# GpSimd makes the folded Fourier input of the second layer, and the first rotary product runs behind the next q's evictions

## The chip, the cores and the metric

The kernel runs on one core of a Trainium2 chip. Its engines are TensorE (PE, with weight loads listed apart as PEld), VectorE (DVE), ScalarE (ACT), GpSimd (POOL) and SyncE (SP, which here only issues DMAs). Each engine works through its own list of instructions in order; semaphores hold an instruction back until what it reads is there. The metric is the device time of one execution, in microseconds (us).

## The reference, cut to what matters

Two layers of an encoder over 272 tokens (16 learned meta tokens and 256 others) with 2048 channels, in float32. Of a layer, the change touches only the way into the projection `f` and into the queries:

```python
h = rmsnorm(x, norm_mix[i])
proj = h @ w_in[i]                      # columns q | k | v | f | ga | gf
q, k: per-head RMS norm over 128 channels, then 2-D rotary:
    concat([x1 * c - x2 * s, x1 * s + x2 * c])      # on each half of the head
f = proj[..., OFF_F:OFF_GA]             # 1024 columns, 8 groups of 128
fr = fft2(f, axes=(tokens, group channels), norm="ortho").real
x = x + (sigmoid(ga) * attn_branch + sigmoid(gf) * (fr @ w_four)) @ w_out
x = x + conv_ffn(rmsnorm(x))
```

The real part of a transform over the tokens needs only the even and the odd part of its input about the middle. So the second layer projects for `f` not `h` but its sums and differences `h[n] + h[T-n]` and `h[n] - h[T-n]`, up to 138 columns each: the *folded* input (`fw` is the weight prepared for it in memory).

## The kernel before, in words

**Products in three parts.** Every weight streams from memory in chunks of 512 KB, tile `raw` (128 x 1024 numbers, four blocks of 128 contraction rows by 256 columns, or in `f4` one contraction block by 1024 columns), issued by SP (L264) into five buffers. Of each chunk ACT makes a rounded copy `wh` (L303) and DVE the remainder `wl` (L306, which waits for that copy); each has four buffers and is made up to three chunks ahead. The activations are split the same way, into `xH` and `xL`. PE adds up `wh*xH`, `wh*xL` and `wl*xH`. Nearly everything else is done in the shadow of these products.

**The order of the work.** Side work is written as Python generators on a list. At each step of the product loops the code takes the next piece of them: `yield n` means "go on in n steps", and `until(hold, flag)` runs them until a flag is set. A scheduler then fixes the order of instructions on each engine from that program, except where a stretch is marked `manual_schedule`; there the order is the one written. DVE has such a stretch around the second q chunk and the folded projection of layer 2, and ACT around that q's evictions and the folded projection.

**The order in layer 2** is k, v, q0, q1, f4, q2, q3 and the gates. `f4` is the folded projection: 16 contraction blocks (k = 0 to 15, chunks 448 to 463 from a weight named `fw`), on each of which PE runs products of `wh` and `wl` with the folded input of that block (L845, L849). Chunk 447 is the last of q1.

**The folded input.** `rstdB` is the tokens' normalising factor, broadcast over partitions; it is ready shortly before layer 2's v. Unit b of eight covers contraction blocks 2b and 2b+1 and has four operations: `t1 = XT * rstdB` (L781, 128 x 544 numbers), the sum (L783, 128 x 274), the difference (L784, 128 x 276), and a copy of the two unpaired columns (L785, 128 x 4). Then, for each block, ACT makes the rounded, scaled part (L788) and DVE its remainder (L795), in one of eight slots, five of which lie in tile `hA` and three in `hB`. Units 0 to 3 are made ahead, in the steps of v and q0 (`fold_ahead`); units 4 to 7 within f4 into slots that are then free, one in three blocks. `t1`, `hf` and most other scratch tiles of this stage (`qp`, `qps`, `qs`, `kp`, `kps`, and later `cf` and `sg`, the constants of the Fourier transform over channels) share one tag of seven buffers.

**Around the change.** `head_evac` empties a q or k product from PSUM (L912 on ACT for the squares, L913 on DVE, into `qp`). `swap` moves halves of heads about by four DMAs into `qs`. `rope` is three DVE products (L930 to L932), an ACT cast (L933) and a DVE subtraction (L935). `kstats` makes the keys' norm: sums by DVE into `kss` (L921, L956, L957), POOL's power `rk` (L515), six scalings `dk` by DVE (L964), and on PE a product of `dk` with ones, `ps_kb` (L967), that stands in PE's list ahead of the last products of v. `pn` are the attention's probabilities, which POOL scales later (L1086).

The manual stretch reads:

```python
                if last and i == 1:
                    until(hold, "ahead")
                    with tc.manual_schedule(engines={mybir.EngineType.DVE}):
                        ps = group((l, "q", i), xr(lo), W)
                        with tc.manual_schedule(engines={mybir.EngineType.Activation}):
                            qq = head_evac(ps, prm[:, P_QN + l:P_QN + l + 1], "qp", lo)
                            qq += (swap(qq[0]),)
                            folded_f(slots, E)
```

Of the kernel before, what the change touches and what calls it, by code (L numbers as in the profile page):

```python
# [13 lines left out]
ALU = mybir.AluOpType  # L14
# [6 lines left out]
T = NM + SEQ  # L21
DEPTH = 2
KT = D // P
# [54 lines left out]
TH = T // 2 + 2  # L78
# [100 lines left out]
def encoder_kernel(ctx, tc, xT, params, consts, bmat, cfold, csign, w_fl, w_f64c, w_in, w_abr, w_four, w_f64, w_out, w_up, w_down, w_vn, w_dn, w_dt, out):  # L179
    nc = tc.nc  # L180
# [12 lines left out]
    for l in range(DEPTH):  # L193
# [42 lines left out]
    for key, chs in order:  # L236
        for j, ch in enumerate(chs):
            n = 0
# [58 lines left out]
    def split_w(i, a, b, parts="hl"):  # L297
        if i not in splits:
            splits[i] = split_tiles(i)
        h, lo = splits[i]  # L300
        r = raws[i]
        if "h" in parts:
            nc.scalar.copy(h[:, a:b], r[:, a:b])  # L303
        st["wl"] = lo
        if "l" in parts:
            nc.vector.tensor_tensor(lo[:, a:b], r[:, a:b], h[:, a:b].bitcast(F32), op=ALU.subtract)  # L306
            if b == CW:
                del raws[i]
# [25 lines left out]
    def until(hold, flag):  # L334
        while flag not in hold:
            step(True)
# [173 lines left out]
    def bc2(ap):  # L510
        return _rep(ap, 2)
# [99 lines left out]
    for l in range(DEPTH):  # L611
# [4 lines left out]
        hold = {}  # L616

        with tc.tile_pool(name=f"mix{l}", bufs=1) as mp:
# [159 lines left out]

            def fold_sum(b, slots):
                t1 = rt("t1")  # L780
                nc.vector.tensor_tensor(t1, XT[:, 2 * b:2 * b + 2, :], bc2(rstdB), op=ALU.mult)  # L781
                hf = rw("hf").rearrange("p k (e n) -> p k e n", e=2)
                nc.vector.tensor_tensor(hf[:, :, 0, 1:TH], t1[:, :, 1:TH], t1[:, :, T - 1:T - TH:-1], op=ALU.add)  # L783
                nc.vector.tensor_tensor(hf[:, :, 1, :], t1[:, :, 1:TH + 1], t1[:, :, T - 1:T - TH - 1:-1], op=ALU.subtract)  # L784
                nc.scalar.copy(hf[:, :, 0, 0:T // 2 + 1:T // 2], t1[:, :, 0:T // 2 + 1:T // 2])  # L785
                for q in range(2):
                    k = 2 * b + q
                    nc.scalar.activation(slots[k % NS][:, :, 0, :], hf[:, q], AF.Copy, scale=prm[:, P_NM + l * KT + k:P_NM + l * KT + k + 1])  # L788
                return hf

            def fold_low(b, slots, hf):
                for q in range(2):
                    k = 2 * b + q
                    sl = slots[k % NS]
                    nc.vector.scalar_tensor_tensor(sl[:, :, 1, :], hf[:, q], prm[:, P_NM + l * KT + k:P_NM + l * KT + k + 1],  # L795
                                                   sl[:, :, 0, :].bitcast(F32), op0=ALU.mult, op1=ALU.subtract)

            def fold_ahead(slots):
                yield 9
                for b in range(NS // 2):  # L800
                    hf = fold_sum(b, slots)
                    yield 2
                    fold_low(b, slots, hf)
                    yield 1
                hold["ahead"] = True

            def folded_f(slots, E):
                assert order[st["grp"]][0] == (l, "f4")
                st["grp"] += 1
                ps = {}  # L810
                for g in (0, 1, 2, 3):
                    ps[g] = [psum.tile([P, 512], F32, tag="aux" if g < 2 else "mm", name=f"ps_f{g}{e}") for e in range(2)]
                p64 = ps[0][0][:2 * NG, 2 * TH:3 * TH]
                hf = None
                wx = {}
                for k in range(KT):
                    i = st["next"]
                    advance(i + 1 + LOOK)
                    ahead = [j for j, _ in todo]
                    todo.clear()  # L820
                    if k < KT - 1:
                        for j in ahead:
                            split_w(j, 0, CW, "h")
                    if hf is not None:
                        fold_low(hf[0], slots, hf[1])
                        hf = None
# [12 lines left out]
                    for q, g in kg:  # L839
                        h, lo_, sl = wx[q]  # L840
                        for e in range(2):
                            w = slice(e * P, (e + 1) * P)
                            o2 = st2(ps[g][e][:, :2 * TH].rearrange("p (r n) -> p r n", r=2))
                            x = al(sl[:, e])
                            nc.tensor.matmul(o2, h[:, g, w], x, start=q == 0, stop=False)  # L845
                            if g == e == 0:
                                for r in range(2):
                                    nc.tensor.matmul(p64, w64s[:, q, :], sl[:, 0, r, :], start=False, stop=False)
                            nc.tensor.matmul(st2(ps[g][e][:, :TH]), lo_[:, g, w], x[:, 0], start=False, stop=q == KT - 1)  # L849
                        if k == KT - 1:  # L850
                            for e in range(2):
                                ev = hv(E[:, g, e, :])
                                nc.scalar.copy(ev, de(ps[g][e][:, TH:2 * TH]))
                                nc.vector.tensor_tensor(ev, de(ps[g][e][:, :TH]), ev, op=ALU.add)
                            if g == 3:
                                for j in ahead:
                                    split_w(j, 0, CW)
                            if g == 0:
                                nc.scalar.copy(e64, p64)
# [66 lines left out]
                    tc.keep_in_program_order(nc.sync.dma_start(qs[32 * b:32 * b + 32, :, :], hp[32 * (b ^ 1):32 * (b ^ 1) + 32, :, :]))  # L926
                return qs

            def rope(hp, qs, H, L):
                tc.keep_in_program_order(nc.vector.tensor_tensor(qs, qs, bc2(sin), op=ALU.mult))  # L930
                tc.keep_in_program_order(nc.vector.tensor_tensor(hp, hp, bc2(cos), op=ALU.mult))
                nc.vector.tensor_tensor(hp, hp, qs, op=ALU.add)  # L932
                nc.scalar.copy(H, hp)  # L933
                yield 1
                nc.vector.tensor_tensor(L, hp, H.bitcast(F32), op=ALU.subtract)  # L935
# [77 lines left out]
            def q_stage(i, qp, qsq, qs):  # L1013
                kv, j = i // 2, i % 2
                sl = slice(2 * j, 2 * j + 2)
                if j == 0:
                    qvs.append(small.tile([P, 9], F32, tag="qv", name="qv"))
                    qsms.append(small.tile([P, 2, 4, NM], F32, tag="sqm", name="sqm", bufs=2))
                qv, qsm = qvs[kv], qsms[kv]
                yield 5  # L1020
                nc.vector.tensor_copy(qsm[:, :, 2 * j:2 * j + 2, :], qsq[:, :, 0:NM].unsqueeze(1).to_broadcast([P, 2, 2, NM]))
                d4 = qv[:, 4 * j:4 * j + 4]
                sums_t(d4, [qsq[:, m, a:b] for m in range(MG) for a, b in BLK[1:]])
                d4 = d4.rearrange("p (m i) -> p m i", m=2)
# [9 lines left out]
                yield from rope(qp, qs, qH[kv][:, sl, :], qL[kv][:, sl, :])  # L1034
# [536 lines left out]
```

## Time and profile before

| | |
|---|---|
| time, median of 3 runs | 2376.45 us (2375.04 to 2378.63) |
| profiled execution | 2377.1 us, span 2375.2 us, granted TensorE clock 0.999 |
| PE busy | 2357.5 us, 99% of the span |
| DVE, ACT, POOL busy | 1802.9, 1313.3, 191.5 us (76%, 55%, 8%) |
| memory traffic | 660.70 MB, mean 278 GB/s |

The profile is of one execution. The page gives the busy time of each engine; the lists of waits say how long an engine stood idle before an instruction and which engine's work ended that; timelines give start and duration of single instructions. A busy figure for PE says only that an instruction was running: at half the granted clock it is as busy and takes longer, so the tables by windows (sum of the window, then busy us and instruction count of PE, PEld, DVE, ACT and POOL, then the granted clock as a share of full speed, the busy share of the DMA engines, and GB/s) have to be read beside it.

### The profile page before, as it was taken

The page shows a single profiled execution, that of the slowest core. Times are in us where ns is not written, and L with a number is a line of the kernel's source. Part 1 is how long each engine was busy: PE and PEld are TensorE (multiplying, and loading weights), DVE is VectorE, ACT ScalarE, POOL GpSimd, SP SyncE. Part 2 cuts the span into 40 slices and gives each one's busy share as a digit, 9 for nine tenths or more (in the row PEclk, how much of TensorE's full clock was granted, in tenths as well). Part 3 has the DMA queues.
Part 4 walks back from the last instruction along what each step waited for, and adds up shares of the span by engine and source line. Part 5 has one row for each costly group of instructions (what it writes and reads, how often), then busy time and mean ns, then how long its engine had stood idle before and what let it go on. Part 6 is the DMA issues. An engine that isn't in the chain of part 4 may idle for free. (4 is left out here: it accounts for less than half of the span.)

```text
span 2375.2 us, 47690 instructions
## 1 busy us (share of the span) xinstructions
PE 2357.5 (99%) x18992; PEld 2305.7 (97%) x18992; DVE 1802.9 (76%) x2813; ACT 1313.3 (55%) x1929; POOL 191.5 (8%) x303
## 2 busy tenths in 40 slices
PE   9999999999999999999999999999999999999999
PEld 9999999999999999999999999999999999999998
DVE  7787867877777556767568877676888889888798
ACT  6565544554444334444455665445676666666575
POOL 0022110000000000000000131000010000000000
PEclk9999999999999999999999999999999999999999
DMA  7557999989999999999886546888889989988887
GB/s 268 178 165 229 305 297 318 294 285 337 319 316 309 320 325 328 309 322 310 263 261 202 182 151 217 263 287 256 285 303 307 323 291 307 306 305 282 258 283 264
DMA packets 171217, 660.70 MB, mean 278 GB/s; under 512 B 19425, under 2 KB 24673, under 8 KB 170097
## 3 DMA queue, kind: packets, MB, share of 16 engines
q1 hardware_dynamic: 152528, 538.07, 64.5%
q0 software_dynamic: 17024, 117.45, 19.7%
q8 instruction: 149, 2.44, 0.4%
q10 hardware_dynamic: 1440, 2.13, 0.3%
q14 instruction: 76, 0.61, 0.1%
HBM read 635.91 MB, written 136.31 MB: 325 GB/s over the span
## 5 line engine op out<-in xcount | busy, mean ns | idle before, releaser
L306 DVE TENSOR_TENSOR wl<-raw,wh 128x1024 fp32r<-128x1024 f32 (+1 forms) x937 | 1129.4, 1218 | 463.4 <-ACT wh L303 449.7
L303 ACT CAST wh<-raw 128x1024 fp32r<-128x1024 f32 (+1 forms) x937 | 966.3, 1041 | 717.2 <-PE ps_ug L376 192.3
L377 PE MATMUL ps_ug<-xHL,wl 128*128 128x272 f32 (+1 forms) x1408 | 390.3, 277 | 0.6 <-DVE wl L306 0.6
L375 PE MATMUL ps_ug<-xHL,wh 128*128 128x272 f32 (+1 forms) x1408 | 390.8, 278 | 0.0
L376 PE MATMUL ps_ug<-xHL,wh 128*128 128x272 f32 (+1 forms) x1408 | 390.0, 277 | 0.0
L376 PEld LDWEIGHTS ps_ug<-xHL,wh 128*128 128x128 f32 x1408 | 267.4, 190 | 2.1
L375 PEld LDWEIGHTS ps_ug<-xHL,wh 128*128 128x128 f32 x1408 | 267.4, 190 | 2.1
L377 PEld LDWEIGHTS ps_ug<-xHL,wl 128*128 128x128 f32 x1408 | 267.5, 190 | 1.0 <-DVE wl L306 1.0
L377 PE MATMUL ps_d<-gHL,wl 128*128 128x272 f32 x704 | 196.4, 279 | 0.0
L375 PE MATMUL ps_uv<-xHL,wh 128*128 128x272 f32 x704 | 196.4, 279 | 0.0
L376 PE MATMUL ps_d<-gHL,wh 128*128 128x272 f32 x704 | 196.4, 279 | 0.0
L376 PE MATMUL ps_uv<-xHL,wh 128*128 128x272 f32 x704 | 196.4, 279 | 0.0
L375 PE MATMUL ps_d<-gHL,wh 128*128 128x272 f32 x704 | 196.4, 279 | 0.0
L377 PE MATMUL ps_uv<-xHL,wl 128*128 128x272 f32 x704 | 196.4, 279 | 0.0
L1414 PE MATMUL ps_p<-wh,opnd 128*128 128x512 f32 x688 | 177.1, 380 | 0.0
L560 POOL COPY tick<-wl 128x1 f32<-128x1 f32 x112 | 38.1, 340 | 1501.7 <-DVE wl L306 1476.9
L371 PE MATMUL ps_uv<-xHL,wh 128*128 128x512 f32 x448 | 149.9, 382 | 0.0
L375 PE MATMUL ps_ga<-xHL,wh 128*128 128x272 f32 (+1 forms) x512 | 143.9, 281 | 0.0
L376 PE MATMUL ps_o<-mL,wh 128*128 128x272 f32 (+1 forms) x512 | 141.9, 277 | 1.4 <-DVE mL L1228 1.4
L375 PE MATMUL ps_gf<-xHL,wh 128*128 128x272 f32 (+1 forms) x512 | 143.2, 280 | 0.0
L376 PE MATMUL ps_gf<-xHL,wh 128*128 128x272 f32 (+1 forms) x512 | 141.8, 277 | 0.0
L377 PE MATMUL ps_gf<-xHL,wl 128*128 128x272 f32 (+1 forms) x512 | 141.8, 277 | 0.0
(371 smaller groups left out, 5989.9 us busy)
## 6 DMA issues: line engine op xcount, KB each, us to landing
raw<-in_w_up SPq DMA_DIRECT2D x320, 512.0 KB, 5.6
raw<-in_w_in SPq DMA_DIRECT2D x191, 512.0 KB, 4.4
raw<-in_w_down SPq DMA_DIRECT2D x88, 512.0 KB, 6.6
raw<-ft SPq DMA_DIRECT2D x80, 512.0 KB, 5.1
raw<-in_w_out SPq DMA_DIRECT2D x64, 512.0 KB, 6.1
ft<-in_w_dn POOLq DMA_DIRECT2D x30, 1024.0 KB, 12.1
raw<-in_w_dn SPq DMA_DIRECT2D x60, 512.0 KB, 5.0
raw<-in_w_abr SPq DMA_DIRECT2D x32, 512.0 KB, 4.8
```

Of the source, the lines that this page charges most:

```text
L303: nc.scalar.copy(h[:, a:b], r[:, a:b])
L306: nc.vector.tensor_tensor(lo[:, a:b], r[:, a:b], h[:, a:b].bitcast(F32), op=ALU.subtract)
L371: nc.tensor.matmul(o2, h[:, c, sl], ab, start=kt == 0, stop=False)
L375: nc.tensor.matmul(o, h[:, c, sl], a, start=kt == 0, stop=False)
L376: nc.tensor.matmul(o, h[:, c, sl], b, start=False, stop=False)
L377: nc.tensor.matmul(o, lo[:, c, sl], a, start=False, stop=kt == nk - 1)
L560: tc.keep_in_program_order(nc.gpsimd.tensor_copy(tick, st["wl"][:, 0, 0:1].bitcast(F32)))
L1414: nc.tensor.matmul(st2(ps[h]), x, al(w[:, 512 * h:512 * h + 512]), start=fresh and (s_, q) in BEGIN and first, stop=(s_, q) in END and end ...
```

## The change

Four operations of each folded unit move to POOL: three from DVE, the copy from ACT. The ACT part gets a function of its own, `fold_high`. Units 4 to 7 are started one in two blocks and not one in three. The rotary product of q0 no longer runs where the scheduler had put it, in q1's last chunk; it is held until f4 and done in three pieces at blocks 0, 1 and 2, behind that block's splits.

```diff
             def fold_sum(b, slots):
                 t1 = rt("t1")
-                nc.vector.tensor_tensor(t1, XT[:, 2 * b:2 * b + 2, :], bc2(rstdB), op=ALU.mult)
+                nc.gpsimd.tensor_tensor(t1, XT[:, 2 * b:2 * b + 2, :], bc2(rstdB), op=ALU.mult)
...
-                nc.vector.tensor_tensor(hf[:, :, 0, 1:TH], t1[:, :, 1:TH], t1[:, :, T - 1:T - TH:-1], op=ALU.add)
-                nc.vector.tensor_tensor(hf[:, :, 1, :], t1[:, :, 1:TH + 1], t1[:, :, T - 1:T - TH - 1:-1], op=ALU.subtract)
-                nc.scalar.copy(hf[:, :, 0, 0:T // 2 + 1:T // 2], t1[:, :, 0:T // 2 + 1:T // 2])
+                nc.gpsimd.tensor_tensor(hf[:, :, 0, 1:TH], t1[:, :, 1:TH], t1[:, :, T - 1:T - TH:-1], op=ALU.add)
+                nc.gpsimd.tensor_tensor(hf[:, :, 1, :], t1[:, :, 1:TH + 1], t1[:, :, T - 1:T - TH - 1:-1], op=ALU.subtract)
+                nc.gpsimd.tensor_copy(hf[:, :, 0, 0:T // 2 + 1:T // 2], t1[:, :, 0:T // 2 + 1:T // 2])
+                return hf
+
+            def fold_high(b, slots, hf):
                 for q in range(2):
                     k = 2 * b + q
                     nc.scalar.activation(slots[k % NS][:, :, 0, :], hf[:, q], AF.Copy, scale=prm[:, P_NM + l * KT + k:P_NM + l * KT + k + 1])
...
             def fold_ahead(slots):
-                yield 9
+                yield 5
                 for b in range(NS // 2):
                     hf = fold_sum(b, slots)
-                    yield 2
+                    yield 3
+                    fold_high(b, slots, hf)
+                    yield 1
                     fold_low(b, slots, hf)
                     yield 1
...
             def folded_f(slots, E):
...
                     if k < KT - 1:
                         for j in ahead:
                             split_w(j, 0, CW, "h")
-                    if hf is not None:
-                        fold_low(hf[0], slots, hf[1])
-                        hf = None
-                    if k % 3 == 2 and k < 3 * (KT - NS) // 2:
-                        hf = NS // 2 + k // 3, fold_sum(NS // 2 + k // 3, slots)
+                    b = NS // 2 + k // 2
+                    if k % 2:
+                        if b < KT // 2:
+                            sums[b] = fold_sum(b, slots)
+                        if b - 1 in sums:
+                            fold_high(b - 1, slots, sums[b - 1])
+                    elif b - 2 in sums:
+                        fold_low(b - 2, slots, sums[b - 2])
                     if k < KT - 1:
                         for j in ahead:
                             split_w(j, 0, CW, "l")
+                    if k < 3:
+                        hold["turn"] = k
+                        until(hold, ("roped", k))
...
-            def rope(hp, qs, H, L):
+            def rope(hp, qs, H, L, apart=False):
...
                 nc.vector.tensor_tensor(hp, hp, qs, op=ALU.add)
+                if apart:
+                    yield 1
                 nc.scalar.copy(H, hp)
...
+                if last and i == 0:
+                    while "turn" not in hold:
+                        yield 3
+                    for n, _ in enumerate(rope(qp, qs, qH[kv][:, sl, :], qL[kv][:, sl, :], True)):
+                        hold["roped", n] = True
+                        yield 1
+                    hold["roped", 2] = True
+                else:
+                    yield from rope(qp, qs, qH[kv][:, sl, :], qL[kv][:, sl, :])
```

Lines of the changed kernel are numbered a little higher (the first q's rotary L930 becomes L940, `head_evac` L912 and L913 become L922 and L923, `dk` L964 becomes L976, the ACT part L788 becomes L791, the remainder L795 becomes L797). In the rows below, `wh440` is the rounded copy of chunk 440, the number behind it tells instances apart.

At the start of layer 2's v, ACT's list holds, before, one unit's two casts and then the copies of chunks 440 and 441:

```order
L912 ACTIVATE kps_16004<-ps_1_k_0_1_15862 128x272
L785 COPY hf_16122<-t1_16120 128x2x2
L788 ACTIVATE hA_16013<-hf_16122,prm_71 128x2x138 x2
L303 CAST wh440_16070<-raw440_15863 128x1024
L303 CAST wh441_16100<-raw441_15893 128x1024
L785 COPY hf_16156<-t1_16154 128x2x2
```

and now:

```order
L922 ACTIVATE kps_16004<-ps_1_k_0_1_15862 128x272
L791 ACTIVATE hA_16013<-hf_16088,prm_71 128x2x138 x2
L791 ACTIVATE hA_16013<-hf_16146,prm_71 128x2x138 x2
L791 ACTIVATE hA_16013<-hf_16218,prm_71 128x2x138
L303 CAST wh440_16070<-raw440_15863 128x1024
L791 ACTIVATE hB_16014<-hf_16218,prm_71 128x2x138
L303 CAST wh441_16106<-raw441_15893 128x1024
```

The copy of chunk 440 now stands behind five casts of three units, and chunk 441's behind a sixth.

POOL's list at the same place went from `rk` straight after `tok`, then small memsets, to:

```order
L785 COPY hf_16146<-t1_16144 128x2x2
L781 TENSOR_TENSOR t1_16216<-XT_69,rstdB_80 128x2x272
L783 TENSOR_TENSOR hf_16218<-t1_16216 128x2x137
L784 TENSOR_TENSOR hf_16218<-t1_16216 128x2x138
L785 COPY hf_16218<-t1_16216 128x2x2
L515 TENSOR_TENSOR rk_16060<-kss_16047,mhalf_75 128x6
L781 TENSOR_TENSOR t1_16276<-XT_69,rstdB_80 128x2x272
```

Units 0, 1 and 2 (the first rows show the end of 1 and the whole of 2) stand ahead of the keys' `rk`; unit 3 stands behind it, then the memsets of `qp` and `qps` for q0 and q1, then units 4 to 7.

On DVE at the border from q1 to f4, before, q0's rotary stands ahead of the remainder of chunk 450 and of q1's evictions:

```order
L306 TENSOR_TENSOR wl449_16469<-raw449_16241,wh449_16468 128x1024
L930 TENSOR_TENSOR qs_16379<-qs_16379,cst_72 128x2x272
L931 TENSOR_TENSOR qp_16371<-qp_16371,cst_72 128x2x272
L932 TENSOR_TENSOR qp_16371<-qp_16371,qs_16379 128x2x272
L935 TENSOR_TENSOR q2_16385<-qp_16371,q1_16384 128x544
L306 TENSOR_TENSOR wl450_16504<-raw450_16296,wh450_16503 128x1024
L913 SCALAR_TENSOR_TENSOR qp_16527<-ps_1_q_1_0_16388,prm_71,rstdB_80 128x258
L913 SCALAR_TENSOR_TENSOR qp_16527<-ps_1_q_1_1_16389,prm_71,rstdB_80 128x258
```

and now:

```order
L306 TENSOR_TENSOR wl449_16469<-raw449_16237,wh449_16468 128x1024
L306 TENSOR_TENSOR wl450_16499<-raw450_16282,wh450_16498 128x1024
L923 SCALAR_TENSOR_TENSOR qp_16522<-ps_1_q_1_0_16388,prm_71,rstdB_80 128x258
L923 SCALAR_TENSOR_TENSOR qp_16522<-ps_1_q_1_1_16389,prm_71,rstdB_80 128x258
L1033 COPY sqm_16399<-qps_16523 128x2x32
L306 TENSOR_TENSOR wl451_16546<-raw451_16326,wh451_16545 128x1024
L940 TENSOR_TENSOR qs_16379<-qs_16379,cst_72 128x2x272
L941 TENSOR_TENSOR qp_16371<-qp_16371,cst_72 128x2x272
L942 TENSOR_TENSOR qp_16371<-qp_16371,qs_16379 128x2x272
```

The evictions of q1 moved up past the four rotary instructions.

On SP at f4's end, before, the last chunks of f4 and three of the next weight go out ahead of `cf` and `sg`:

```order
L264 DMA raw461_16678<-fw_66 128x1024
L264 DMA raw462_16710<-fw_66 128x1024
L264 DMA raw463_16736<-fw_66 128x1024
L264 DMA raw464_16760<-in_w_in 128x1024
L264 DMA raw465_16792<-in_w_in 128x1024
L264 DMA raw466_16818<-in_w_in 128x1024
L863 DMA cf_17004<-in_cfold 128x398
L865 DMA sg_17006<-in_csign 16x520
```

and now:

```order
L264 DMA raw461_16684<-fw_66 128x1024
L873 DMA cf_17004<-in_cfold 128x398
L264 DMA raw462_16716<-fw_66 128x1024
L264 DMA raw463_16742<-fw_66 128x1024
L875 DMA sg_17006<-in_csign 16x520
L264 DMA raw464_16774<-in_w_in 128x1024
```

`cf` moved ahead of the last two chunks of f4. Its buffer is one of the seven shared ones, the one that unit 7's `t1` had, so this DMA waits for POOL's last operation of unit 7, and the chunks behind it in the queue wait with it; `sg` follows them and waits for DVE's remainders of unit 6.

More of the change, by code (lines that the diff above doesn't have):

```diff
@@ L788, in fold_sum @@
                     nc.scalar.activation(slots[k % NS][:, :, 0, :], hf[:, q], AF.Copy, scale=prm[:, P_NM + l * KT + k:P_NM + l * KT + k + 1])
-                return hf
             def fold_low(b, slots, hf):
@@ L813, in folded_f @@
                 p64 = ps[0][0][:2 * NG, 2 * TH:3 * TH]
-                hf = None
+                sums = {}
                 wx = {}
@@ L823, in folded_f @@
                             split_w(j, 0, CW, "h")
-                    if hf is not None:
-                        fold_low(hf[0], slots, hf[1])
-                        hf = None
-                    if k % 3 == 2 and k < 3 * (KT - NS) // 2:
-                        hf = NS // 2 + k // 3, fold_sum(NS // 2 + k // 3, slots)
+                    b = NS // 2 + k // 2
[6 more added lines that the diff above has]
+                        fold_low(b - 2, slots, sums[b - 2])
                     if k < KT - 1:
@@ L1033, in q_stage @@
                 yield 4 - j
-                yield from rope(qp, qs, qH[kv][:, sl, :], qL[kv][:, sl, :])
+                if last and i == 0:
[7 more added lines that the diff above has]
+                    yield from rope(qp, qs, qH[kv][:, sl, :], qL[kv][:, sl, :])
                 if j:
```

## The prediction

> **What bounds the kernel now.** I read the page's busy times first, then the list of PE's waits for layer 2's first stage, then windows for the granted clock, then the timelines of PE and DVE around the wait found.
>
> ```profile
> span 2375.2 us, 47690 instructions
> ...
> PE 2357.5 (99%) x18992; PEld 2305.7 (97%) x18992; DVE 1802.9 (76%) x2813; ACT 1313.3 (55%) x1929; POOL 191.5 (8%) x303
> ```
>
> PE bounds the whole. Work taken off DVE or ACT is worth nothing as such; it counts only where PE waits for them. In the stage that the change touches there is one such wait:
>
> ```profile
> PE ps_f L845 <- DVE qp L913: 2.6, 1, 2.6
> ...
> 1279.28 0.28 PE L845 MATMUL ps_f<-hA,wh 128*128 128x276 f32 x1
> 1285.13 0.39 PE L845 MATMUL ps_f<-hA,wh 128*128 128x276 f32 x1 [2.61 <-DVE qp L913]
> 1291.94 0.33 PE L845 MATMUL ps_f<-hA,wh 128*128 128x276 f32 x1
> 1293.96 0.33 PE L845 MATMUL ps_f<-hB,wh 128*128 128x276 f32 x1
> ```
>
> The rows are the start of f4's block 0, the product of block 1 that waits for q1's PSUM, and the starts of blocks 4 and 5. A block takes 1293.96 - 1291.94 = 2.02 us.
>
> ```profile
> 1278.80 1.23 DVE L306 TENSOR_TENSOR wl<-raw,wh 128x1024 fp32r<-128x1024 f32 x1 [0.30 <-issue]
> 1279.94 0.72 DVE L930 TENSOR_TENSOR qs<-qs,cst 128x544 f32<-128x544 f32 x1
> ...
> 1282.82 0.73 DVE L935 TENSOR_TENSOR q<-qp,q 128x544 fp32r<-128x544 f32 x1 [0.77 <-ACT q L933]
> 1283.46 1.22 DVE L306 TENSOR_TENSOR wl<-raw,wh 128x1024 fp32r<-128x1024 f32 x1
> 1284.59 0.87 DVE L913 SCALAR_TENSOR_TENSOR qp<-ps_q,prm,rstdB 128x258 f32<-128x258 f32 x2
> ```
>
> On DVE, q0's rotary runs from 1279.94 to 1283.55, and q1's evictions, for which PE waits, come behind it. The clock shows what the wait costs besides:
>
> ```profile
> 1286.00:1287.00 1.00, 1.00 (x7) 0.92 (x7) 0.70 (x2) 1.00 (x2) 0.00 (x0) 0.52 0.80 295
> ...
> 1288.00:1289.00 1.00, 1.00 (x6) 1.00 (x6) 0.97 (x3) 0.00 (x0) 0.00 (x0) 0.50 0.63 166
> ...
> 1290.00:1291.00 1.00, 1.00 (x12) 0.98 (x11) 1.00 (x2) 1.00 (x3) 0.00 (x0) 1.00 0.99 389
> ```
>
> The number after POOL's (x0) is the granted clock: about half from 1286 to past 1289, with 6 or 7 products per us against 12.
>
> **Term 1, the rotary moved behind the evictions: a gain of 4.6 us.** Unstalled, block 5 would start at 1279.28 + 5 x 2.02 = 1289.38; it starts at 1293.96, so the wait and its half clock cost 4.58 (2.61 idle, 1.97 clock). After the change, DVE's list has the remainders of chunks 449 and 450 (1.22 each, from 1278.80), then the evictions (0.87): done by 1282.1, and PE asks at 1285.13 - 2.61 = 1282.52. The wait goes, if only by 0.4 us. The rotary itself costs nothing more: q0's result is wanted only by the attention, past f4. What it delays on DVE are the remainders of chunks 451 to 453, made three chunks (6 us) ahead; three products of 0.72 fit in that.
>
> **The price of a unit on POOL.** A unit took 1.6 us of DVE, and POOL shows no product of two tensors of this size:
>
> ```profile
> L781 DVE TENSOR_TENSOR t<-XT,rstdB x8: 715/718/726, 1243.6 to 1306.4; 128x544 f32<-128x544 f32 x8
> ...
> L783 DVE TENSOR_TENSOR hf<-t x8: 439/445/448, 1244.4 to 1307.2; 128x274 f32<-128x274 f32 x8
> ...
> L784 DVE TENSOR_TENSOR hf<-t x8: 436/440/442, 1244.7 to 1307.5; 128x276 f32<-128x276 f32 x8
> ```
> ```profile
> L495 POOL MEMSET V<- 128x256 f32 x1 | 0.3, 315 | 0.0
> L1011 POOL MEMSET pn<- 128x128 f32 x8 | 1.3, 206 | 8.2 <-ACT xHL L519 8.2
> L1086 POOL TENSOR_SCALAR pn<-pn,rs 128x384 f32<-128x384 f32 x36 | 55.4, 1540 | 130.9 <-ACT pn L1080 67.0 <-DVE rs L1085 45.1 <-PE ps_pt L1093 7.0
> ...
> L1086 POOL TENSOR_SCALAR pn<-pn,rs x36: 1237/1245/2332, 127.5 to 1436.2; 128x384 f32<-128x384 f32 x36
> ...
> L560 POOL COPY tick<-wl x112: 175/184/4247, 190.8 to 2070.1; 128x1 f32<-128x1 f32 x112
> ```
>
> Lower end: the memsets give (315 - 206)/128 = 0.85 ns a number and 0.1 us a start; for 1094 numbers in three operations and a copy, 1.4 us. The nearest row reads and computes: L1086, undisturbed 1.24 us for 384 numbers; with the 0.18 of the one-number copy as its start, (1.24 - 0.18)/384 = 2.76 ns a number. 544, 274 and 276 numbers then take 1.68, 0.94 and 0.94, with the copy 3.74; neighbours overlap a little, so 3.5. Upper end: a second tensor doubles the price a number, 6.6. I take U = 3.5. The Trainium skill, "GPSIMD Engine Reference", on tensor_tensor against the Vector engine, measures 4497 ns against 2293 (1.96 times) for 2048 numbers; on DVE's rows an estimate of 3.3 us a unit, and a sum lower by 1.2 us than mine. No run here shows a tensor_tensor of that size on POOL.
>
> POOL also waits while DVE reads two tensors:
>
> ```profile
> 1403.63 1.23 DVE L306 TENSOR_TENSOR wl<-raw,wh 128x1024 fp32r<-128x1024 f32 x1
> ...
> 1403.82 2.15 POOL L1086 TENSOR_SCALAR pn<-pn,rs 128x384 f32<-128x384 f32 x1 [16.87 <-ACT pn L1080]
> ```
>
> A POOL operation begun 0.2 us into a remainder ends 0.9 late. On the mean L1086 is 1.54 - 1.24 = 0.30 above its least, amid remainders on DVE; I take 0.3 an operation, 1.2 a unit, in f4, and a third of that ahead of f4, where only one remainder and two fold remainders fall into the stretch.
>
> **Term 2, the keys' norm waits for POOL: a loss of 5.4 us, and 1.5 of clock.** The rows of the stage before:
>
> ```profile
> 1242.76 0.39 ACT L603 COPY rstdB<-ps_nb 128x272 f32<-128x272 f32 x1
> 1245.49 0.94 ACT L788 ACTIVATE hA<-hf,prm 128x276 fp32r<-128x276 f32 x2
> 1246.81 1.05 ACT L303 CAST wh<-raw 128x1024 fp32r<-128x1024 f32 x1 [0.38 <-PE ps_v L376]
> ...
> 1248.73 1.22 DVE L306 TENSOR_TENSOR wl<-raw,wh 128x1024 fp32r<-128x1024 f32 x1
> 1250.61 1.45 POOL L515 TENSOR_TENSOR rk<-kss,mhalf 128x6 f32<-128x6 f32 x1 [9.46 <-DVE kss L957]
> 1252.09 0.62 DVE L964 TENSOR_SCALAR dk<-cst,rk 128x16 f32<-128x16 f32 x3 [1.21 <-POOL rk L515]
> ...
> 1255.03 0.62 PE L967 MATMUL ps_kb<-dk,ones 128*128 128x272 f32 x2
> ```
>
> `rstdB` is there at 1243.15. Before, the first `dk` was done at 1252.71, and PE took `ps_kb` in its turn at 1255.03: 2.3 us of slack. Now ACT's copy of chunk 440 stands behind casts of units 0, 1 and 2, DVE's remainder of that chunk behind the copy, and `kss`, `rk` and `dk` behind the remainder. Unit 2 ends at E2 = 1243.15 + 3 x 3.5 + 1.2 = 1254.85. Then 0.53 for the last cast, 1.05 for the copy, and the old distance from the remainder's start to the end of `dk`, 1252.71 - 1248.73 = 3.98: `ps_kb` at E2 + 5.56 = 1260.4. PE idles 5.4 us there, with the last six products of v and all of q0 behind it in its list. After that idle the clock falls as it did in f4; I take 1.5, between none and f4's 1.97:
>
> ```profile
> 1370.00:1380.00 10.00, 8.47 (x74) 8.14 (x73) 9.72 (x20) 6.56 (x16) 2.49 (x2) 1.00 0.45 150
> ```
>
> Here 1.5 us of idle, in pieces, cost no clock; a single 5.4 is nearer to f4's 2.61. Ends: U = 1.4 gives E2 = 1248.6, no idle; U = 6.6 gives 14.7.
>
> **Term 3, f4's last chunks wait for `cf`: a loss of 1.9 us.**
>
> ```profile
> 1288.17 12.62 SPq L264 DMA_DIRECT2D raw<-fw  x8
> ...
> 1306.91 0.43 SPq L863 DMA_DIRECT2D cf<-in_cfold  x1
> ...
> raw<-fw SPq DMA_DIRECT2D x12, 512.0 KB, 4.2
> ```
>
> Before, all of f4's chunks had been issued by 1300.79 and `cf` came late. Now SP holds chunk 462 (block 14) behind `cf`, and `cf` behind POOL's last operation of unit 7 at E7. Chunk 462's remainder is then ready at E7 + 0.43 (issue of `cf`) + 4.2 (landing) + 1.05 + 1.22 = E7 + 6.9; PE starts block 14 at 1279.28 + 14 x 2.02 = 1307.56. Unit 4's sum waits for q0's rotary, which has its buffer: from the evictions' end at 1282.1, the small `sqm`, a remainder and three products end at about 1285.5; sum, difference and copy add 2.0, with waiting 3.0: E4 = 1288.5. A unit then takes 3.5 + 1.2 = 4.7, longer than the 4.04 of two blocks, so E7 = 1288.5 + 3 x 4.7 = 1302.6, and PE idles 1302.6 + 6.9 - 1307.56 = 1.9. Ends: nothing for U under 2.9 (E7 at 1300.7), 11 for 6.6. ACT's copies stand behind the casts of the units too, but three chunks ahead, which covers what a unit is late until about the seventh.
>
> What DVE and ACT no longer do (1.6 and 0.2 us a unit) is worth nothing: PE waits for neither elsewhere in the stage.
>
> **Sum.** -4.6 + 5.4 + 1.5 + 1.9 = +4.2 us on the profiled execution's 2377.1, of which 1.9 lie around its span. That execution is 0.65 above the median, 2376.45; the median becomes 2380.7. A measurement tells about 0.2% from no change, here 4.75 us: the forecast lies just inside, and U decides it, at 6 us for each us of U.
>
> **Rivals.**
>
> *POOL is fast enough, and the gain stands.* With U at 1.7 or less (E2 at 1249.45) terms 2 and 3 are nothing, and 2376.45 - 4.6 = 2371.9 remains. For it: the memset's 0.85 ns a number. Against: every reading row of POOL costs three times that. Between 1.7 and 2.6 the loss is smaller than the gain.
>
> *POOL and DVE exclude each other.* The row at 1403.82 waits nearly as long as DVE's operation lasts. If each always holds the other off, two blocks cost DVE 2 x 1.22 for remainders, 2 x 0.5 for the fold's, plus POOL's 3.5: 6.9 us against PE's 4.04. E7 becomes 1288.5 + 3 x 6.9 = 1309.2 and term 3 is 8.5, so +10.8, or 2387.3. Against: the median of L1086 is within 8 ns of its least, so over half of these were not held at all. The Trainium skill, "SBUF — State Buffer", on the port that the two share, has it as this lock, for a DVE instruction with two inputs against a POOL one that reads; the 2.15 us agrees, the median does not tell.
>
> *A second tensor doubles POOL's price*, U = 6.6: terms 2 and 3 are 14.7 + 1.9 and 11, or 2400.
>
> *The wait at f4's start stays.* The margin is 0.4 us; if unit 4's product holds DVE's evictions, the 4.6 is not won: 2385.
>
> **How the numbers follow.** The forecast's case (U from 2.6 to 4.3, -1 to +9) has 0.60; POOL fast 0.16; exclusion 0.14; doubled price 0.04; the wait stays 0.06. Of the forecast's case half lies above +4.75: 0.27, with the last three slower, 0.51 slower. Faster by 0.2% needs the whole gain and some luck: 0.07. Within, 0.42. The range leaves out the doubled price, the fastest POOL and the worst of exclusion: 2372.5 to 2387.5; the forecast's own is 2375 to 2385.
>
> **What would show it.** PE's wait for `qp` gone from f4's start, evictions done near 1282 (term 1). POOL's L781 near 1.7 us, its sums near 0.9 (U). An idle of PE ahead of `ps_kb`, released by `dk`, with half a clock behind it (term 2). `cf` on SP ahead of chunk 462 and past 1302, PE idle at block 14 for its copy or remainder (term 3). Wrong: L781 near 0.6 us, or DVE's remainders stretched to 2 us while POOL runs, or PE's next wait at another place, such as the casts of units 5 to 7 on ACT.

## The result, and the profile after

The changed kernel takes 2387.13 us in the median (2386.69 to 2389.83, 5 runs), the kernel before beside it 2378.08; the ratio on record is 1.0049, with an interval from 1.0038 to 1.0059. (It is not the quotient of the two medians, which is 1.0038.) By the medians the loss is 9.05 us, by the ratio 11.7, by the spans of the two profiled executions 11.8. The forecast was 4.2 us of loss, 2380.7 in a range from 2372.5 to 2387.5: the sign is right, the loss more than twice the size, and the median just inside the range's upper end.

The page of the kernel after, its span, busy times, and then the list of PE's waits in layer 2's first stage:

```profile
span 2387.0 us, 47685 instructions
...
PE 2360.1 (99%) x18992; PEld 2307.1 (97%) x18992; DVE 1802.3 (76%) x2789; ACT 1311.8 (55%) x1921; POOL 224.5 (9%) x335
```
```profile
PE ps_kb L979 <- DVE dk L976: 5.4, 1, 5.4
PE ps_f L859 <- DVE wl L306: 3.3, 4, 1.0
PE ps_q L375 <- DVE E L864: 1.9, 1, 1.9
```

The wait for `qp` is gone, and three others have come. DVE's busy time is the same as before although twenty-four operations left it: most of what it saved came back as longer instructions.

What a wait costs with its slower clock is read from a ledger: the start of the same PE product in the timelines of both executions, and the difference between them. (f4's first product, for example, starts at 1287.74 and not at 1279.28, which is 8.46 late.) It is 0.45 us in v, ahead of the last six products, and changes at four places only:

| place on PE | late at its end, us | change |
|---|---|---|
| v, ahead of its last six products | 0.45 | |
| the keys' norm (`ps_kb`) and the half clock behind it, up to f4's start | 8.46 | +8.01 |
| f4's blocks 0 to 3 | 3.83 | -4.63 |
| f4's blocks 4 to 14 | 7.19 | +3.36 |
| block 15, the border to q2, and q2's first chunk | 12.12 | +4.93 |

From there on it stays at 12.1 to the last gate compared.

**The keys' norm.** Timelines of POOL (first, last and behind), ACT, DVE and PE:

```profile
1243.39 1.36 POOL L781 TENSOR_TENSOR t<-XT,rstdB 128x544 f32<-128x544 f32 x1 [2.08 <-ACT rstdB L603]
...
1253.54 0.19 POOL L785 COPY hf<-t 128x4 f32<-128x4 f32 x1
1257.13 1.51 POOL L515 TENSOR_TENSOR rk<-kss,mhalf 128x6 f32<-128x6 f32 x1 [3.40 <-DVE kss L969]
1258.63 1.32 POOL L781 TENSOR_TENSOR t<-XT,rstdB 128x544 f32<-128x544 f32 x1
...
1253.77 0.53 ACT L791 ACTIVATE hA<-hf,prm 128x276 fp32r<-128x276 f32 x1 [2.05 <-POOL hf L785]
1254.20 1.03 ACT L303 CAST wh<-raw 128x1024 fp32r<-128x1024 f32 x1
...
1255.26 1.22 DVE L306 TENSOR_TENSOR wl<-raw,wh 128x1024 fp32r<-128x1024 f32 x1 [4.36 <-ACT wh L303]
1258.68 3.25 DVE L976 TENSOR_SCALAR dk<-cst,rk 128x16 f32<-128x16 f32 x6 [1.23 <-POOL rk L515]
...
1261.02 1.25 PE L979 MATMUL ps_kb<-dk,ones 128*128 128x272 f32 x2 [5.39 <-DVE dk L976]
```

This is the chain of the forecast, link by link: three units on POOL, the cast, the copy of chunk 440, its remainder (DVE idle 4.36 for it), `kss`, `rk`, `dk`, `ps_kb`. The windows show the clock behind it:

```profile
1260.00:1265.00 5.00, 3.98 (x16) 3.78 (x17) 5.00 (x10) 1.05 (x1) 1.80 (x5) 0.50 0.05 11
1265.00:1270.00 5.00, 5.00 (x39) 4.92 (x39) 4.41 (x9) 1.04 (x1) 0.00 (x0) 0.88 0.81 264
```

**f4.** First the wait of unit 4 for the rotary and its end, then unit 6 as an example, POOL, DVE and ACT apart. (The row names a DMA as the releaser; q0's third rotary product ended at 1292.55, and in this kernel, in pool_only, pool_late and late_own_cf unit 4's sum starts 0.13 to 0.14 us after that product.)

```profile
1292.68 1.66 POOL L783 TENSOR_TENSOR hf<-t 128x274 f32<-128x274 f32 x1 [7.17 <-DMA qs<-qp]
...
1296.06 0.68 POOL L785 COPY hf<-t 128x4 f32<-128x4 f32 x1
...
1302.11 2.21 POOL L781 TENSOR_TENSOR t<-XT,rstdB 128x544 f32<-128x544 f32 x1
1304.41 0.85 POOL L783 TENSOR_TENSOR hf<-t 128x274 f32<-128x274 f32 x1
1305.22 0.97 POOL L784 TENSOR_TENSOR hf<-t 128x276 f32<-128x276 f32 x1
1306.14 1.19 POOL L785 COPY hf<-t 128x4 f32<-128x4 f32 x1
1307.40 2.22 POOL L781 TENSOR_TENSOR t<-XT,rstdB 128x544 f32<-128x544 f32 x1
...
1303.04 2.52 DVE L797 SCALAR_TENSOR_TENSOR hA<-hf,prm,hA 128x276 fp32r<-128x276 f32 x2
1305.48 2.92 DVE L306 TENSOR_TENSOR wl<-raw,wh 128x1024 fp32r<-128x1024 f32 x2
...
1307.36 0.53 ACT L791 ACTIVATE hA<-hf,prm 128x276 fp32r<-128x276 f32 x1 [2.46 <-POOL hf L785]
```

From one `t` to the next POOL takes 1307.40 - 1302.11 = 5.29 us, against 4.04 for PE's two blocks. Ahead of f4 a whole unit took 3.0 (1250.69 to 1253.73); here the copy of four numbers lasts 1.19 and not 0.19, and DVE's fold remainders 1.26 each and not 0.50. Neither engine has a gap worth the name. ACT's copies stand behind the unit's cast, which waits 2.46 us for POOL, but they are not what comes late in blocks 9 and 11: the copy of chunk 457 (block 9) was done at 1303.94, and DVE, busy all the time, came to its remainder at 1305.48.

The end of f4, on SP, ACT, DVE and PE (its waits in blocks 9, 11, 14, 15 and at q2's start):

```profile
1312.63 0.33 SPq L873 DMA_DIRECT2D cf<-in_cfold  x1
1313.07 0.85 SPq L264 DMA_DIRECT2D raw<-fw  x2
...
1316.93 1.05 ACT L303 CAST wh<-raw 128x1024 fp32r<-128x1024 f32 x1 [2.42 <-DMA raw<-fw]
1320.24 1.05 ACT L303 CAST wh<-raw 128x1024 fp32r<-128x1024 f32 x1 [2.26 <-DMA raw<-fw]
...
1318.01 1.23 DVE L306 TENSOR_TENSOR wl<-raw,wh 128x1024 fp32r<-128x1024 f32 x1 [2.24 <-ACT wh L303]
...
1322.65 1.28 ACT L843 ACT_TABLE_LOAD   x1
1324.99 0.79 ACT L863 COPY E<-ps_f 128x138 f32<-128x138 f32 x4
...
1307.33 0.33 PE L859 MATMUL ps_f<-hA,wl 128*128 128x138 f32 x1 [0.99 <-DVE wl L306]
1312.61 0.33 PE L859 MATMUL ps_f<-hA,wl 128*128 128x138 f32 x1 [1.03 <-DVE wl L306]
1319.29 0.33 PE L859 MATMUL ps_f<-hB,wl 128*128 128x138 f32 x1 [0.40 <-DVE wl L306]
1322.60 0.33 PE L859 MATMUL ps_f<-hB,wl 128*128 128x138 f32 x1 [0.87 <-DVE wl L306]
1326.61 0.38 PE L375 MATMUL ps_q<-xHL,wh 128*128 128x258 f32 x1 [1.90 <-DVE E L864]
```

`cf` goes out when unit 7 is done (1312.62), and chunks 462 and 463 behind it. Their copies and the next chunk's are late on ACT, the table load for the attention's exponential comes behind them, and only then come f4's evictions, for which q2 waits.

### The profile page after: what moved, and what is told of

Its sections match the earlier page's. It is cut to its first block, busy times and chain, and to the rows that moved or that the text cites. A ratio compares the mean times of both kernels' runs of the same rounds, so it can differ in the third digit from the quotient of the medians.

```text
span 2387.0 us, 47685 instructions
## 1 busy us (share of the span) xinstructions
PE 2360.1 (99%) x18992; PEld 2307.1 (97%) x18992; DVE 1802.3 (76%) x2789; ACT 1311.8 (55%) x1921; POOL 224.5 (9%) x335
## 4 chain that ended last, share of the span: by engine, by line
PE 93%; DVE 3%; DMA 1%; ACT 1%; issue 1%; POOL 0%; SPq 0%; DVEq 0%; ACTq 0%; POOLq 0%
PE ps_p L1434 11%; PE ps_ug L376 7%; PE ps_ug L377 7%; PE ps_ug L375 7%; PE ps_uv L371 4%; PE ps_d L377 3%; PE ps_uv L376 3%; PE ps_uv L375 3%; PE ps_uv L377 3%; PE ps_d L376 3%; PE ps_d L375 3%; PE ps_o L376 2%; PE ps_o L377 2%; PE ps_o L375 2%; PE ps_ga L376 2%; PE ps_ga L375 2%
## 5 line engine op out<-in xcount | busy, mean ns | idle before, releaser
L375 PE MATMUL ps_gf<-xHL,wh 128*128 128x272 f32 (+1 forms) x512 | 143.2, 280 | 0.0
L377 PE MATMUL ps_ga<-xHL,wl 128*128 128x272 f32 (+1 forms) x512 | 141.8, 277 | 0.0
L377 PE MATMUL ps_o<-mH,wl 128*128 128x272 f32 (+1 forms) x512 | 141.8, 277 | 0.0
```

The source lines that it names most:

```text
L375: nc.tensor.matmul(o, h[:, c, sl], a, start=kt == 0, stop=False)
L377: nc.tensor.matmul(o, lo[:, c, sl], a, start=False, stop=kt == nk - 1)
```

## The experiments

All times are medians beside runs of the kernel before; the stage columns are changes of the ledger against the kernel before (norm: v's end to f4's start; f4 start: blocks 0 to 3; f4: blocks 4 to 14; end: from block 15 into q2). Each column is read from one profiled execution: after, pool_only and pool_ahead have the same three units ahead of the keys' norm and read 8.0, 7.5 and 7.5, so half a microsecond there is scatter. The executions also differ by -1.6 to +2.8 us ahead of this stage, which the columns leave out. Where the interval holds 1 (ahead_two, ahead_one, late_own_cf) the median does not tell the kernel from the one before, and what is said of it rests on the ledger and the lists of waits.

| kernel | median | before | ratio (interval) | norm | f4 start | f4 | end |
|---|---|---|---|---|---|---|---|
| after | 2387.13 | 2378.08 | 1.0049 (1.0038, 1.0059) | +8.0 | -4.6 | +3.4 | +4.9 |
| rope_only | 2372.81 | 2376.84 | 0.9987 (0.9978, 0.9996) | 0.0 | -4.6 | 0.0 | +1.2 |
| pool_only | 2384.51 | 2376.84 | 1.0037 (1.0025, 1.0050) | +7.5 | -1.2 | 0.0 | 0.0 |
| pool_late | 2379.74 | 2376.84 | 1.0019 (1.0010, 1.0027) | 0.0 | -4.6 | +4.7 | +4.2 |
| pool_ahead | 2379.81 | 2376.84 | 1.0012 (1.0004, 1.0021) | +7.5 | -4.6 | 0.0 | +0.1 |
| ahead_two | 2376.63 | 2376.87 | 1.0002 (0.9992, 1.0011) | +4.6 | -4.6 | 0.0 | +0.1 |
| ahead_one | 2374.25 | 2376.87 | 0.9992 (0.9983, 1.0002) | -0.1 | -3.7 | +0.5 | +1.2 |
| late_own_cf | 2376.96 | 2376.87 | 1.0006 (0.9997, 1.0015) | 0.0 | -4.6 | +4.0 | 0.0 |
| beside_read | 2382.03 | 2376.87 | 1.0019 (1.0009, 1.0029) | 0.0 | -4.6 | +10.6 | 0.0 |
| beside_write | 2372.93 | 2376.99 | 0.9984 (0.9975, 0.9993) | 0.0 | -4.6 | +0.1 | +1.2 |
| rope_warm | 2373.67 | 2376.99 | 0.9984 (0.9975, 0.9993) | 0.0 | -4.6 | 0.0 | +0.1 |

**rope_only: the rotary move alone.** Units made as before, in the old steps.

```diff
-                nc.gpsimd.tensor_tensor(t1, XT[:, 2 * b:2 * b + 2, :], bc2(rstdB), op=ALU.mult)
+                on_pool = False
+                eng = nc.gpsimd if on_pool else nc.vector
+                eng.tensor_tensor(t1, XT[:, 2 * b:2 * b + 2, :], bc2(rstdB), op=ALU.mult)
...
-                yield 5
+                yield 9
```

> Only the rotary move; the folded units stay on DVE and ACT as before, one in three blocks, with the old steps ahead. Ledger theory (each delay on PE has its own place: 8.5 us at the keys' norm, -4.6 at the start of f4, 8.3 at the end of f4): only the -4.6 is left, so 2372 to 2374 us, no idle of PE at f4's start, no half clock there. Rival (the rotary's three products do not fit behind the evictions, where DVE already has fold units and remainders, so f4 loses them again): no gain, within 1 us of before, PE waiting for a remainder in f4.

4.63 us are won at f4's start, as forecast, and 1.2 given back at q2, which neither theory had. The list of PE's waits:

```profile
PE ps_q L375 <- DVE E L863: 1.0, 1, 1.0
```

No remainder is late in f4, so the rival falls.

**pool_only: the move to GpSimd alone.** The rotary as before.

```diff
-                    if k < 3:
+                    if False:
                         hold["turn"] = k
                         until(hold, ("roped", k))
...
-                if last and i == 0:
+                if False:
                     while "turn" not in hold:
```

> Only the move to GpSimd (with its new steps); q0's rotary stays where it was, in q1's last chunk. Additive theory (the terms are independent): the kernel after plus 4.6, about +16 us on before. Rival (unit 4 is late only because its sum waits for the held rotary): GpSimd starts f4's units about 8 us earlier, f4's end loses nothing, and the sum is the 8.5 of the keys' norm alone plus at most 2, 2385 to 2388, with the old 2.6 us wait at f4's start back.

The rival holds: f4 loses nothing. Unit 4's sum follows the rotary's end here as well, but at 1288.87, with the rotary in q1:

```profile
1288.87 0.77 POOL L783 TENSOR_TENSOR hf<-t 128x274 f32<-128x274 f32 x1 [3.32 <-DVE qp L942]
```
```profile
PE ps_kb L979 <- DVE dk L976: 5.4, 1, 5.4
PE ps_f L855 <- DVE qp L923: 1.4, 1, 1.4
```

That is 3.8 us earlier than in the kernel after, and block 4 comes 3.4 later: 7.2 us more time for the units. They are no faster for it (from unit 5's `t` at 1291.95 to unit 6's at 1298.02 it is 6.07 us); they have slack. So the two parts of the change interact: the late units in f4 are the price of the moved rotary together with GpSimd, not of either alone. The old wait is back, at 1.4 us for 2.6; f4's start is 1.2 us better than before. The median, 2384.51, lies half a microsecond under the rival's 2385 to 2388.

**pool_late and pool_ahead: GpSimd for one half of the units each**, the rotary moved. DVE and ACT make the other half in the old steps.

```diff
+                on_pool = b >= NS // 2          # pool_late; b < NS // 2 in pool_ahead
+                eng = nc.gpsimd if on_pool else nc.vector
-                nc.gpsimd.tensor_tensor(t1, XT[:, 2 * b:2 * b + 2, :], bc2(rstdB), op=ALU.mult)
+                eng.tensor_tensor(t1, XT[:, 2 * b:2 * b + 2, :], bc2(rstdB), op=ALU.mult)
```

> The rotary moved, GpSimd makes units 4 to 7 alone; units 0 to 3 on DVE and ACT with the old steps. Ledger theory: -4.6 at f4's start, +8.3 at f4's end, nothing at the keys' norm: +3.7, 2380 to 2382, E7 (GpSimd's last operation) about 25 us after f4's start. Rival (f4's loss comes from chunks already late from the first stage): f4 loses nothing and the time is that of the rotary move alone.

> The rotary moved, GpSimd makes units 0 to 3 alone; units 4 to 7 on DVE and ACT as before, one in three blocks. Ledger theory: +8.5 at the keys' norm, -4.6 at f4's start, nothing at f4's end: +3.9, 2380 to 2382, PE idle 5.4 us ahead of ps_kb. Rival (the idle at ps_kb lets loads and splits run ahead, so that q0, q1 and f4 give part of it back): below 2379.

PE's waits, of pool_late and then of pool_ahead:

```profile
PE ps_f L860 <- DVE wl L306: 3.8, 4, 1.2
PE ps_q L375 <- DVE E L865: 1.9, 1, 1.9
```
```profile
PE ps_kb L979 <- DVE dk L976: 5.4, 1, 5.4
```

Each shows its own loss whole and not the other's; both rivals fall, though both medians come out 0.2 to 0.3 under the 2380 to 2382 expected. Norm, f4 and end of the two together, 7.5 + 4.7 + 4.2 + 0.1, less 4.6, make 11.9, against 11.7 for after. (In pool_late unit 7 ended 26.4 us after f4's start, 1304.03 - 1277.68, where 25 was expected.)

**ahead_two and ahead_one: fewer units ahead of the keys' norm.** pool_ahead with one number changed, which moves POOL's third unit (and second) behind `rk`, and their casts behind the copy of chunk 440.

```diff
             def fold_ahead(slots):
-                yield 5
+                yield 9                         # ahead_two; 16 in ahead_one
```

> GpSimd makes units 0 to 3, the rotary is moved, units 4 to 7 stay on DVE (pool_ahead), but the units start four steps later, so that two and not three of them stand ahead of the keys' rk on GpSimd and ahead of chunk 440's copy on ACT. Queue theory (ps_kb waits for whatever GpSimd has ahead, 3.0 us a unit): the idle ahead of ps_kb falls from 5.4 to about 2.4 us and the loss of that stage from 7.4 to about 4; total 2376 to 2378. Rival (GpSimd's reading slows DVE's own work there, wherever the units stand): the idle stays above 4 us.

> As ahead_two, but units start eleven steps later, so that only unit 0 stands ahead of rk and of chunk 440's copy. Queue theory: no idle ahead of ps_kb, the stage loses nothing, and the time is that of the rotary move alone, 2372 to 2374. Rival (slowed DVE): an idle of 3 us or more at ps_kb or in q0, above 2376.

The idle ahead of `ps_kb`, with three, two and one unit ahead, is 5.4, 2.8 and none, a step of 2.6 for a unit of 3.0 us:

```profile
PE ps_kb L979 <- DVE dk L976: 2.8, 1, 2.8
```

The loss goes with the units in the queue, and the rival of a general slowing falls. In ahead_one units 1 to 3 run later instead (the last ends at 1278.40, 1.4 us before f4 starts), and f4's two columns are 0.9 and 0.5 us worse than in rope_only; no single wait explains that, the list has two for remainders of 0.5 us together. At the end of the stage it is 2.1 us ahead of the kernel before, and rope_only 3.4.

**late_own_cf: `cf` and `sg` in a buffer of their own**, one that layer 2 doesn't use, so that they are loaded long before.

```diff
-                cf = rw("cf").rearrange("p a b -> p (a b)")
+                own = wp.tile([P, CW, MG * P], F32, tag="wpm", name="own", bufs=1).rearrange("p a b -> p (a b)")
+                cf = own[:, 0:400]
...
-                sg = rw("sg").rearrange("p a b -> p (a b)")[:2 * NG, :CW * 2 * HC1]
+                sg = own[:2 * NG, 400:400 + CW * 2 * HC1]
```

> pool_late (rotary moved, GpSimd makes units 4 to 7), but cf and sg have a buffer of their own and are loaded long before, so no weight chunk waits behind them. Theory of cf (the forecast's third term): PE's idle at blocks 13 and 15 and most of the 4.2 us between f4's end and q2 go, total near 2373 to 2375. Rival (GpSimd and DVE take turns, 5.3 us for two blocks that PE does in 4.04): the waits for remainders in blocks 8 to 13 stay, 3 to 4 us, and at most 3 us of the end are won: 2376 to 2378.

Against pool_late the end falls from +4.2 to 0.0 and f4 from +4.7 to +4.0: 4.9 us in all were the queue behind `cf`. The waits for remainders in f4 stay:

```profile
PE ps_f L860 <- DVE wl L306: 3.3, 3, 1.2
```

Both theories hold a part: `cf` was worth more than the rival's 3 us by the ledger (2.8 by the medians), and the rest is as the rival says. (The profiled execution took 2379.57, 2.6 above the median; it was 2.8 late ahead of v's last chunk and gained 0.7 from there on.)

**beside_read and beside_write: what GpSimd does to DVE by running beside it.** rope_only, with extra GpSimd work in f4 that nothing reads.

```diff
+                    if k in (1, 3, 5, 7):
+                        nc.gpsimd.tensor_copy(own[:, 0:1], st["wl"][:, 0, 0:1].bitcast(F32))
+                        nc.gpsimd.tensor_tensor(d1, XT[:, 2 * d:2 * d + 2, :], bc2(rstdB), op=ALU.mult)
+                        nc.gpsimd.tensor_tensor(d2[:, :, 0, 0:119], d1[:, :, 1:120], d1[:, :, T - 1:T - 120:-1], op=ALU.add)
+                        nc.gpsimd.tensor_tensor(d2[:, :, 1, 0:119], d1[:, :, 1:120], d1[:, :, T - 1:T - 120:-1], op=ALU.subtract)
```

and in beside_write, in place of the three products and sums:

```diff
+                        for _ in range(4):
+                            nc.gpsimd.memset(own, 0.0)
```

> rope_only (units on DVE), and beside it GpSimd does four extra units in f4 at blocks 1, 3, 5 and 7 that nothing reads: one small copy, one product of 544 and two sums of 238 numbers a row into a buffer of their own. Lock theory (an operation of GpSimd that reads and one of DVE with two inputs from memory on the chip take turns): DVE's remainders stretch from 1.22 to about 1.45 us on the mean and its fold remainders to 1 us and more, DVE falls behind, and f4 loses 3 to 8 us against rope_only, 2376 to 2381. Rival (only the queue order behind the units costs): DVE's durations stay and the time is that of rope_only, 2372 to 2374.

> As beside_read, but of GpSimd's extra work in f4 (blocks 1, 3, 5, 7) only the one-number copy reads; the rest is four fills of 1024 numbers a row, about 0.9 us each by the fills seen before (3.6 us a round, as long as the reading unit). Lock theory for reading operations: fills do not hold DVE off, its remainders stay at 1.22 us, f4 as in rope_only, 2371 to 2374. Rival (any operation of GpSimd takes turns with DVE, or GpSimd's activity as such costs): DVE's durations stretch as in beside_read and f4 loses 5 to 10 us.

DVE's groups in a window of f4 (the line's operation, how many, busy time and mean duration), of beside_read and then of beside_write:

```profile
L306 DVE TENSOR_TENSOR wl<-raw,wh 128x1024 fp32r<-128x1024 f32 x9 | 13.9, 1562 | 0.0
L786 DVE TENSOR_TENSOR hf<-t 128x276 f32<-128x276 f32 x3 | 4.8, 1589 | 0.0
```
```profile
L306 DVE TENSOR_TENSOR wl<-raw,wh 128x1024 fp32r<-128x1024 f32 x13 | 15.5, 1220 | 0.2
```
```profile
1285.86 3.98 POOL L844 MEMSET own<- 128x1024 f32 x4
```

Beside GpSimd's reading sums a remainder takes 1.56 us on the mean and a difference of 276 numbers 1.59, not 0.44; f4 loses 10.6, more than the 3 to 8 expected, and the median, 2382.03, is over 2381. Beside fills, which kept GpSimd busy for 4.0 us a round, nothing is longer and the ledger is that of rope_only to 0.1 us. So it is not GpSimd's being busy nor a queue behind it that holds DVE off, but that its operations read (they also compute, which a fill does not; the two runs do not part these). The Trainium skill, "SBUF — State Buffer", section "Who interferes with whom", puts it down to the reading: a DVE instruction with two inputs from SBUF, the memory on the chip, contends with a GpSimd instruction that reads SBUF, not with one that only writes it. Both halves agree here, with 1.56 and 1.220 us a remainder.

**rope_warm: the table load moved.** rope_only with ACT's small exponential at block 10.

```diff
-                    if k == 13:
+                    if k == 10:
                         nc.scalar.activation(warm, mhalf[:, 0:1], AF.Exp)
```

> rope_only with ACT's small exponential, which loads its table ahead of the attention, at f4's block 10 instead of 13. In rope_only that load (1.28 us) and the copy of chunk 464 behind it stand ahead of f4's evictions, DVE's adds come behind that chunk's remainder, and PE waits 1.0 us for them ahead of q2 (1.16 of the 4.6 won are given back). Theory: the load fits into ACT's idle 1.6 us ahead of unit 7, the wait goes, 1.2 us less than rope_only: 2370 to 2372, PE's gain at q2 4.6 and not 3.4. Rival (the evictions wait for the chunk's copy itself, not for the table): no difference from rope_only.

```profile
1301.91 1.28 ACT L842 ACT_TABLE_LOAD   x1
...
1308.96 0.96 ACT L862 COPY E<-ps_f 128x138 f32<-128x138 f32 x4 [0.28 <-PE ps_f L858]
```

The evictions now wait for PE and not PE for them; the 1.2 us come back, 5.54 us ahead at q2 where the execution was 0.99 ahead at v's end. By the ledger this is the best of the kernels here. By its time it can't be told from rope_only: 1.1 us lie within the scatter, and its median came out 0.9 higher, outside the 2370 to 2372 expected.

## Why the prediction was right in part and wrong in size

- **Term 1** (-4.6): measured -4.63. Right. The margin of 0.4 us is read in rope_only, where PE is not late: the evictions end at 1280.78, and PE's old request falls at 1282.52 - 1.16 = 1281.36, a margin of 0.6. In the kernel after it is 2.1 (1288.85 against 1282.52 + 8.46 = 1290.98), since DVE has both remainders done when the late q1 ends.
- **Term 2** (+5.4 idle, +1.5 clock): 5.39 idle, 2.6 clock (8.01 - 5.39). The place and chain were right, the 5.4 was luck. A unit takes 3.0 us and not 3.5, so unit 2 ended at 1253.73, 1.1 earlier than forecast. But of the six `dk` scalings, which took 3.25 us beside unit 3's reading product and sum, the first three, for which `ps_kb` waits, took 2.2 where they had taken 0.62: the distance from unit 2's end to `ps_kb` was 7.29 and not 5.56. So `ps_kb` came at 1261.02, 0.6 later than forecast, and PE had itself come 0.6 later. The clock's part was set between nothing and f4's 1.97, and f4's row was the better guide: in these runs the price does not follow the length of the idle. It is 2.0 us behind an idle of 1.4 (pool_only at f4's start, 4.6 - 1.2 = 3.4 lost), 3.4 behind 2.1 (beside_read, block 11), 1.8 behind 2.8 (ahead_two), 2.1 behind 5.4 (pool_ahead) and 2.6 here.
- **Price of a unit**: the row of 2.76 ns a number was a scaling of another form. 1.35 us for 544 numbers and 0.76 for 274 are about 2.2 ns a number and 0.16 a start. The estimate of 3.3 from the Trainium skill, "GPSIMD Engine Reference", section "3.1 Elementwise — side-by-side cycle accounting", was nearer: for 2048 numbers it has tensor_tensor at 1.96 times DVE's time, and here 2.87 against DVE's 1.60 is 1.8 times.
- **Term 3** (+1.9) is the step that failed: 8.3. E4 came out right (1296.74, less the 8.46 by which f4 starts later, is 1288.3; forecast 1288.5), but by two errors that cancel: unit 4's sum began at 1292.68 - 8.46 = 1284.2 and not at 1285.5, and sum, difference and copy took 4.1 us and not 3.0. From there a unit's time was 5.29 and not 4.7. Chunk 462's remainder was ready 6.6 us after unit 7's end (forecast 6.9), and block 14 waited for it, 0.4 us. Two things were left out.
  - *DVE's side of the exclusion.* The forecast let POOL wait for DVE, 0.3 us an operation, and not DVE for POOL, so that remainders in blocks 9 and 11 held PE up by 2.5 us. "Three chunks ahead, which covers what a unit is late until about the seventh" looked at ACT's copies, which were in time; DVE was what had no time left, and PE waited already behind unit 5.
  - *What stands behind block 14.* The pricing stopped there. Chunk 463, the table load and the evictions behind it cost another 4.9 up to q2, with the clock. In late_own_cf, without the queue behind `cf`, the end loses nothing (4.2 in pool_late), and the waits for remainders stay.
- **The rival of exclusion** (+10.8, chance 0.14) had f4's mechanism. With the measured unit full exclusion gives 3.44 + 3.04 = 6.5 us for two blocks, and 5.29 were measured. The single records of unit 6 show where the 1.2 us are: POOL's four operations and DVE's two remainders and two fold remainders end in turn, and each ends behind the one before it by its undisturbed time less 0.13 to 0.20 us (the product 1.21 behind a remainder, about 1.35 undisturbed; the copy 0.05 for 0.19; the next remainder 1.09 for 1.22). That the rival came near in time is luck: it had 8.5 us lost by block 14, where 3.4 were, and the rest was lost behind. The undisturbed median of L1086 was taken against it. In the trace before, each of the 12 of these 36 operations that took 1.9 us and more had a remainder beside it for 0.8 us or more, the other 24 for 0.62 at most; so the median says nothing of f4, where DVE has no gap.
- The sum of the terms was 4.2; the span grew by 11.8. Of the 7.6 between them 6.4 are term 3 and 1.1 is the clock of term 2. (In the chances, half of 0.60 is 0.30 and not 0.27.)

## What to carry to other kernels

Work moved to an idle engine is priced by what stands behind it in every queue that reads its result: here an ACT copy behind a cast and a weight DMA behind a buffer cost more than the operations. GpSimd is no spare VectorE for work on two tensors, since in f4 each held the other off; where DVE is full, count its time onto DVE's, less the little that overlapped here (0.13 to 0.20 us an operation). And follow a delay past its first victim: the last chunk, the table load and the evictions behind the one priced cost more than it did.

## What the runs showed of the hardware that was not expected

- The hold goes both ways and is not only for large operations or those on two tensors: a GpSimd copy of four numbers a row took 1.19 us in place of 0.19, and six DVE scalings of one tensor each 3.25 in place of 1.3 (0.62, 0.42 and 0.29 before).
- GpSimd's fills of 1024 numbers a row, 1.0 us each, left DVE's remainders at 1.220 us.
- An idle of PE of 1.4 us (pool_only, f4's start) was followed by half the granted clock, 0.50, and cost as much beyond itself, 2.0 us, as one of 2.6 us before (1.97). Idles of 1.0 us (rope_only at q2) and 1.3 us (beside_read, block 9) left the clock at 1.00.
